# Gated linear attention: decay levels multiplied one head at a time, in half the rows, instead of two heads through a zero-padded operand

## The chip, the cores and the metric

The kernel runs on one core of one Trainium2 chip. The metric is device time of one launch in microseconds (us), the median of several runs. The engines are called PE (TensorE), DVE (VectorE), ACT (ScalarE), POOL (GpSimd) and SP (SyncE); PEld are PE's weight loads.

## The reference

A trunk of two layers over 512 positions of width 2048. Each layer normalises its input, projects it with one combined matrix, runs three head groups in parallel (a gated short convolution, stick-breaking attention with 8 heads, gated linear attention, GLA, with 4 heads of 64 keys and 128 values), multiplies each by a SiLU gate and projects the concatenation back into the residual stream. The GLA part, which is what changes:

```python
def step(state, inp):
    qc, kc, vc, gc = inp
    cum = jnp.cumsum(gc, axis=2)
    o_inter = jnp.einsum("bhck,bhkv->bhcv", qc * jnp.exp(cum), state)
    diff = cum[:, :, :, None, :] - cum[:, :, None, :, :]
    decay = jnp.where(causal, jnp.exp(jnp.minimum(diff, 0.0)), 0.0)
    att = jnp.einsum("bhtk,bhsk,bhtsk->bhts", qc, kc, decay)
    o_intra = jnp.einsum("bhts,bhsv->bhtv", att, vc)
```

and of the convolution `y = b_gate * (conv3(c_gate * h) + bias)`, times `silu(g)`.

## The kernel before

**Projections.** Activations lie in SBUF as two float16 halves (high and low), as do the weights (wh, wl), and every product is three matmuls (high by high, high by low, low by high). Weights come in blocks of 256 columns: POOL issues the load into `st`, ACT finds the sum of squares (L367), POOL reduces it over the partitions (L381), ACT writes wh (L436, L486), DVE writes wl (L443, L487). The plain projections are the matmuls at L673 to L675, L684 to L686 and L815; the ones at L765 and L768 belong to a scheme with seven products instead of eight (`project_quick`), which also needs sums of blocks. Two layers run one after the other: GLA's projections, the first half of the convolution, four pairs of attention heads, the second half of the convolution, the output projection.

**GLA.** Two head pairs p per layer, the two heads of a pair on partitions 0 to 63 and 64 to 127. Within blocks of 128 positions the decay between two positions is split by levels h = 64, 32, ..., 1 (`LEV`): at level h, a source in the first half of a stretch of 2h positions meets a target in the second half, and both decays are taken against the middle, so each factor stays at most 1. At each level DVE and ACT make e (L1045 to L1054), split the source into float16 halves in tile `qp` (`split_src`, L1009 and L1010) and the target into tile `th` (`split_tgt`, L1018 and L1019). The target tile has room for two heads beside each other: head 0's rows fill the columns h = 0, head 1's rows the columns h = 1, and the rest stays at the zeros that POOL wrote at the layer's start (L966). So one matmul over all 128 rows (`mm3`, L1024) gives both heads' scores, 64 target columns each, in one PSUM bank; 4 blocks by 3 terms make 12 of them a level. DVE writes what belongs to the level into `attd` under a mask (L1059). The diagonal comes from a matmul with `heads` (L1073) and a masked write (L1077). Decays between the blocks go through `mm3` with two and four blocks of targets at once, 256 and 512 columns. L1119 multiplies the scores with the values, `norm` (from L1121) normalises and gates.

**The first convolution** runs at the same time as the second head pair: `conv_in` puts h (times its scale) into tile `qT`, multiplies the c projection onto it, and convolves into `kT`; `conv_out` makes the gate in a tile `g`, of which there are two, and multiplies. The GLA gates `gg` hold the same two "g" tiles until their heads are normalised and stored (`mixsplit`).

**What sets the order.** After a start-up whose DVE and ACT order is written by hand, a scheduler that simulates the timeline sets the order of the instructions on each engine, with some priorities and hooks for the weights' preparation. Tiles of one tag share the buffers of that tag, so a tag also sets who waits for whom.

Of the kernel before, what the change touches and what calls it, by code (L numbers as in the profile page):

```python
# [17 lines left out]
P = 128  # L18
# [25 lines left out]
def hybrid_trunk(ctx, tc, x, norm_g, w_in, conv_w, conv_b, sb_qn_g, sb_kn_g,  # L44
# [33 lines left out]
    def wk(shape, tag, bufs=None, dt=F32):  # L78
        return work.tile(shape, dt, tag=tag, name=nm(tag), bufs=bufs)
# [46 lines left out]

    LEV = [64, 32, 16, 8, 4, 2, 1, 0]
    masks = const.tile([P, len(LEV), P], U8, tag="masks", name="masks")

    def make_masks():  # L130
        bits = wk([P, 2, P], "e", dt=I32)
        V.tensor_copy(bits[:, 0, :], colno)
        V.tensor_copy(bits[:, 1, :], pno.to_broadcast([P, P]))
        V.tensor_tensor(bits[:, 0, :], bits[:, 0, :], bits[:, 1, :], ALU.bitwise_xor)
        far = bits[:, 1, :].bitcast(F32)
        V.tensor_copy(far, bits[:, 0, :])
        V.tensor_scalar(bits[:, 1, :], bits[:, 1, :], 0x7F800000, None, ALU.bitwise_and)
        for li, h in enumerate(LEV):
            V.tensor_scalar(masks[:, li, :], far, float(h), None, ALU.is_equal)
# [113 lines left out]
    gmx = sm(depth, "gmx")  # L253
# [33 lines left out]
    def layer_consts():  # L287
# [3 lines left out]
        for l in range(depth):  # L291
# [3 lines left out]
            gq = sm(2, "kg")  # L295
# [239 lines left out]
    ssq = sm(NT * NG, "ssq").rearrange("p (t g) -> p t g", g=NG)  # L535
# [121 lines left out]
    for l in range(depth):  # L657
# [164 lines left out]
        def project_gate(mx=None, logistic=False):  # L822
# [3 lines left out]
            def dst():  # L826
                g.append(wk([P, 2, seq], "g"))
                return g[0]
# [136 lines left out]
        for a in scr:  # L965
            G.memset(a, 0.0)  # L966
        src16 = [[scr[0][:, b, i, :] for i in range(2)] for b in range(2)]
        tgt16 = [[scr[1][:, b, i, :].rearrange("p (t h c) -> p t h c", t=NT, h=2) for i in range(2)] for b in range(2)]
# [5 lines left out]
        for tag in ("qT", "kT"):  # L974
            o = wk([P, 2, seq], tag)
            ps, u = project(True, lambda: o)
            mx = sm(2, tag + "mx")
            for c in range(2):
                V.tensor_reduce(mx[:, c:c + 1], ps[c], AX.X, ALU.max, apply_absolute_value=True)
            gm = allmax(mx, 2, tag)  # L980
            m = sm(1, tag + "m")
            V.tensor_tensor(m, gm[:, 0:1], gm[:, 1:2], ALU.max)
            p2 = sm(1, tag + "p2")
            pow2(p2, m, -14.0, tag)
            s_ = sm(1, tag + "s")
# [26 lines left out]
        def split_tgt(e, b):  # L1012

            for hh in range(2):
                hs = slice(hh * HT, (hh + 1) * HT)
                eh = e[hs].rearrange("p (g c) -> p g c", c=HT)
                hi, lo = (a[hs, :, hh, :] for a in tgt16[b])
                S.activation(hi, eh, AF.Copy)  # L1018
                V.tensor_tensor(lo, eh, hi, ALU.subtract)  # L1019

        def mm3(o, sb, ss, tb, g0, g1):

            for i, (a, b) in enumerate(((0, 0), (0, 1), (1, 0))):
                T.matmul(o, src16[sb][a][:, ss], tgt16[tb][b][:, g0:g1].rearrange("p g h c -> p (g h c)"),  # L1024
                         start=i == 0, stop=i == 2)

        tsl = [slice(t * P, (t + 1) * P) for t in range(NT)]
        for p in range(2):
            Pp, q_, k_ = Pc[:, p, :], gq[:, p, :], gk[:, p, :]
            attd = wk([P, NT, 2, P], "zw")  # L1030
            G.memset(attd, 0.0)

            for li, h in enumerate(LEV[:-1]):
# [25 lines left out]
                V.copy_predicated(  # L1059
                    attd.rearrange("p t h (b s j) -> p (t h) b s j", s=2, j=h)[:, :, :, 1, :],  # L1060
                    masks[:, li, :].rearrange("p (o b s j) -> p o b s j", o=1, s=2, j=h)[:, :, :, 1, :].to_broadcast(
                        [P, 2 * NT, HT // h, h]),
                    aps.rearrange("p (t b j) -> p t b j", t=2 * NT, j=h))
# [7 lines left out]
            for t in range(NT):  # L1071
                for i, a in enumerate((hi, lo)):
# [3 lines left out]
            S.activation(own, aps, AF.Copy, scale=2.0 ** 14)  # L1076
            V.copy_predicated(attd.rearrange("p t h c -> p (t h) c"),  # L1077
                              masks[:, len(LEV) - 1:len(LEV), :].to_broadcast([P, 2 * NT, P]),
# [16 lines left out]
            for i in range(NT):  # L1095
                S.activation(att16[0][:, i], attd[:, i], AF.Copy, scale=2.0 ** -21)
                V.scalar_tensor_tensor(att16[1][:, i], attd[:, i], 2.0 ** -21, att16[0][:, i], ALU.mult, ALU.subtract)
# [7 lines left out]
            for a, o in zip(ax, (aps[:, 0], aps[:, 1], aps2[:, 0])):  # L1105
                S.activation(a[:, 0], o, AF.Copy, scale=2.0 ** -21)
                V.scalar_tensor_tensor(a[:, 1], o, 2.0 ** -21, a[:, 0], ALU.mult, ALU.subtract)
            ops2 = bank2()
            for hh in range(2):
# [3 lines left out]
                for t, cs, a, g0, g1 in ((0, tsl[1], ax[0], 0, 2), (2, tsl[3], ax[0], 2, 4),  # L1113
                                         (0, slice(256, 512), ax[1], 0, 4), (1, slice(256, 512), ax[2], 0, 4)):
                    seqmm.append((cs, t, [a[:, i].rearrange("p (g h c) -> p g h c", h=2, c=HT)[:, g0:g1, hh, :]
# [28 lines left out]
        def weight_ratio():  # L1144
# [8 lines left out]
            rp = sm(1, "rpm")  # L1153
# [10 lines left out]
        def conv_in(j, then=lambda: None):  # L1164
# [23 lines left out]
            return y  # L1188

        def conv_out(j, y, then=lambda: None):  # L1190

            g, u = project_gate(logistic=j == 1)
# [21 lines left out]
        conv_out(0, conv_in(0, lambda: norms.pop(0)()))  # L1214
# [70 lines left out]
        for j in range(4):  # L1285
# [15 lines left out]
            m = sm(1, "sbm")  # L1301
# [5 lines left out]
            for n in range(2):  # L1307
# [20 lines left out]
                u2 = sm(1, "qu2")  # L1328
# [28 lines left out]
        conv_out(1, conv_in(1, go), go)  # L1357
# [7 lines left out]
        if not last:  # L1365
            xt = [newbig("x", [P, 2, D], F32, l) for _ in range(2)]
            ssq = sm(NT * NG, "ssq").rearrange("p (t g) -> p t g", g=NG)
# [76 lines left out]
```

## Time and profile before

| | |
|---|---|
| median of 3 runs | 1662.28 us (1662.23 to 1664.69) |
| profiled execution | 1665.0 us, of which the span from the first to the last instruction 1663.1 us |
| granted TensorE clock, mean | 0.997 |
| PE matmuls, weight loads | 17098 each |
| DVE, ACT busy | 1393.4 us, 1181.9 us |
| DMA | 232.71 MB, mean 140 GB/s |

Busy time is the union of an engine's records. Matmuls are pipelined, so a record of a matmul is longer than the distance to the next one's start; rates are read from starts.

### The profile page before, as it was taken

To read this page: it belongs to the slowest core of one execution; us is meant where nothing else is said; L and a number is where in the kernel's file an instruction comes from. 1 tells how busy PE (TensorE), PEld (TensorE's weight loads), DVE (VectorE), ACT (ScalarE), POOL (GpSimd) and SP (SyncE) were. 2 spreads that over 40 slices of the span, in tenths; PEclk is the share of its full clock that TensorE was granted. 3 is DMA by queue.
4 is the path that set the end of the run, shared out by engine and by line. 5 is a ranking of instruction groups with operands and counts; after the bars stand their busy time and mean duration, and the time that the engine had idled before them with its cause. 6 is when DMAs were issued, how large, how long until landed. Compare 5 with 4: busy or idle time off the path is not lost.

```text
span 1663.1 us, 39967 instructions
## 1 busy us (share of the span) xinstructions
PE 1637.7 (98%) x17098; PEld 1327.7 (80%) x17098; DVE 1393.4 (84%) x2347; ACT 1181.9 (71%) x1739; POOL 257.8 (16%) x298
## 2 busy tenths in 40 slices
PE   7999999999999999999999999999999999999999
PEld 5746548989898967799996465689898989668998
DVE  8977789979898979897599686998888888788893
ACT  8667787877777776755675786888786867676571
POOL 1121012111212121011111110112121212111110
PEclk9999999999999999999999999999999999999999
DMA  7144324577776868456433433436677776783441
GB/s 259 52 153 113 102 64 87 132 155 144 162 151 156 157 153 204 154 162 207 163 103 104 112 104 107 121 83 176 115 167 146 160 152 136 155 240 127 153 154 52
DMA packets 189747, 232.71 MB, mean 140 GB/s; under 512 B 90162, under 2 KB 149884, under 8 KB 189056
## 3 DMA queue, kind: packets, MB, share of 16 engines
q0 software_dynamic: 72832, 175.12, 39.0%
q1 hardware_dynamic: 107728, 45.56, 13.4%
q10 hardware_dynamic: 9008, 9.45, 1.7%
q8 instruction: 134, 2.20, 0.5%
q14 instruction: 45, 0.37, 0.1%
HBM read 179.65 MB, written 14.68 MB: 117 GB/s over the span
## 4 chain that ended last, share of the span: by engine, by line
PE 65%; DVE 17%; DMA 8%; issue 4%; ACT 4%; POOL 1%; DVEq 0%; ACTq 0%; POOLq 0%
PE psp L768 14%; PE psp L674 7%; PE psp L673 7%; PE psp L675 7%; PE psp L685 5%; PE psp L686 5%; PE psp L684 5%; PE psp L765 5%; DMA st<-in_w_in_dram 5%; PE psp L815 5%; DMA th<-za 3%; DVE za L1251 2%; DVE wl L487 2%; DVE w7l L487 2%; DVE zw L1253 1%
## 5 line engine op out<-in xcount | busy, mean ns | idle before, releaser
L486 ACT ACTIVATE wh<-st,ws 128x1024 f16<-128x1024 f32 x222 | 247.8, 1146 | 192.2 <-DVE st L507 100.5
L487 DVE SCALAR_TENSOR_TENSOR wl<-st,ws,wh 128x1024 f16<-128x1024 f32 x222 | 279.6, 1280 | 31.5 <-ACT wh L486 31.2
L367 ACT ACTIVATE junk<-st 128x2048 uint8<-128x2048 f32 x150 | 285.3, 1902 | 12.8 <-DMA st<-in_w_in_dram 7.5
L443 DVE SCALAR_TENSOR_TENSOR wl<-st,ws,wh 128x2048 f16<-128x2048 f32 x78 | 182.8, 2349 | 28.2 <-ACT wh L436 27.1
L685 PE MATMUL psp<-wl,m 128*128 128x256 f16 x704 | 191.9, 273 | 0.0
L684 PE MATMUL psp<-wh,m 128*128 128x256 f16 x704 | 191.9, 273 | 0.0
L686 PE MATMUL psp<-wh,m 128*128 128x256 f16 x704 | 191.9, 273 | 0.0
L436 ACT ACTIVATE wh<-st,ws 128x2048 f16<-128x2048 f32 x76 | 151.0, 1995 | 50.8 <-DVE ws L397 24.2
L768 PE MATMUL psp<-wh,s 128*128 128x128 f16 x2048 | 176.9, 219 | 0.0
L768 PE MATMUL psp<-wl,s 128*128 128x128 f16 x1024 | 173.3, 219 | 0.0
L768 PEld LDWEIGHTS <-s 128*128 128x128 f16 x3072 | 173.1, 98 | 0.0
L381 POOL PARTITION_ALL_REDUCE wgm<-wm x75 | 42.3, 564 | 746.9 <-ACT junk L367 731.7
L355 POOL DMA_DIRECT2D st<-in_w_in_dram x114 | 101.8, 898 | 337.4 <-DVE wl L443 175.1
L765 PE MATMUL psp<-s,wh 128*128 128x256 f16 x896 | 151.9, 273 | 0.0
L765 PEld LDWEIGHTS <-wh 128*128 128x128 f16 x1344 | 131.4, 98 | 16.1 <-issue 1.0
L768 PEld LDWEIGHTS <-m 128*128 128x128 f16 x2160 | 124.3, 99 | 5.5 <-issue 5.0
L765 PE MATMUL psp<-s,wl 128*128 128x256 f16 x448 | 122.0, 273 | 0.0
L675 PEld LDWEIGHTS <-wl 128*128 128x128 f16 x576 | 56.4, 98 | 67.5 <-DVE wl L443 1.6
L675 PE MATMUL psp<-x,wl 128*128 128x512 f16 x288 | 109.0, 379 | 0.4 <-DVE wl L443 0.4
L674 PEld LDWEIGHTS <-wh 128*128 128x128 f16 x576 | 56.4, 98 | 66.3 <-issue 1.3
L674 PE MATMUL psp<-x,wh 128*128 128x512 f16 x288 | 109.2, 379 | 0.0
L674 PE MATMUL psp<-m,wh 128*128 128x512 f16 x288 | 109.2, 379 | 0.0
(426 smaller groups left out, 4195.4 us busy)
## 6 DMA issues: line engine op xcount, KB each, us to landing
st<-in_w_in_dram POOLq DMA_DIRECT2D x114, 1024.0 KB, 8.3
st<-in_w_out_dram POOLq DMA_DIRECT2D x32, 1024.0 KB, 8.4
st<-st POOLq DMA_DIRECT2D x30, 512.0 KB, 7.5
st<-in_w_in_dram SPq DMA_DIRECT2D x6, 1024.0 KB, 11.7
mixd<-g POOLq DMA_DIRECT2D x24, 256.0 KB, 6.2
x<-in_x_dram SPq DMA_DIRECT2D x4, 1024.0 KB, 4.9
qT<-in_x_dram ACTq DMA_DIRECT2D x8, 512.0 KB, 3.7
qT<-xs ACTq DMA_DIRECT2D x8, 512.0 KB, 4.2
```

Source lines behind the costliest of these rows:

```text
L367: sq = S.activation(junk(HK * GW).rearrange("p (k n) -> p k n", k=HK), staged[i][h], AF.Square, accum_out=peak[i][:, h:h + 1])
L436: hi = S.activation(wh[:, :, :GW], staged[i][h], AF.Copy, scale=scales[i])
L443: V.scalar_tensor_tensor(wl[:, :, :GW], staged[i][h], scales[i], wh[:, :, :GW], ALU.mult, ALU.subtract)
L486: hi = S.activation(h_, b, AF.Copy, scale=sc)
L487: V.scalar_tensor_tensor(l_, b, sc, h_, ALU.mult, ALU.subtract)
L674: T.matmul(o, wh[:, kk, cs], xl[:, :, k, :], start=False, stop=False)
L675: mm = T.matmul(o, wl[:, kk, cs], xh[:, :, k, :], start=False, stop=en)
L684: T.matmul(o, ah[:, t, k, :], wh[:, kk, :n], start=st_, stop=False, skip_group_check=True)
L685: T.matmul(o, ah[:, t, k, :], wl[:, kk, :n], start=False, stop=False, skip_group_check=True)
L686: return T.matmul(o, al[:, t, k, :], wh[:, kk, :n], start=False, stop=en, skip_group_check=True)
L765: mm = T.matmul(o, w[q_][:, kk, :], a[p_][:, :, kk, :], start=st_, stop=en, skip_group_check=True)
L768: mm = T.matmul(o[:, t * P:(t + 1) * P], a[p_][:, t, kk, :], w[q_][:, kk, :], start=st_, stop=en, skip_group_check=True)
```

## The change

The target halves become plain tiles of 128 rows and half the columns. `mm3` issues, for each term, one matmul for each head, over that head's 64 rows of source and target, into that head's own PSUM bank. `attd` changes its layout from (block, head, column) to (head, block, column), the masks hold only the second halves of each stretch, four blocks wide, and the diagonal has a mask of its own. Only the source tile is still zeroed. The first convolution's gate is written over its h values. Several small tiles of one to four columns now share tags, among them those of the q and k projections' maxima.

```diff
-    masks = const.tile([P, len(LEV), P], U8, tag="masks", name="masks")
+    masks = const.tile([P, len(LEV) - 1, NT, P // 2], U8, tag="masks", name="masks")
+    mdiag = const.tile([P, P], U8, tag="mdiag", name="mdiag")
...
-        for li, h in enumerate(LEV):
-            V.tensor_scalar(masks[:, li, :], far, float(h), None, ALU.is_equal)
+        for li, h in enumerate(LEV[:-1]):
+            V.tensor_scalar(masks[:, li].rearrange("p t (b j) -> p t b j", j=h),
+                            far.rearrange("p (o b s j) -> p o b s j", o=1, s=2, j=h)[:, :, :, 1, :].to_broadcast(
+                                [P, NT, HT // h, h]), float(h), None, ALU.is_equal)
+        V.tensor_scalar(mdiag, far, 0.0, None, ALU.is_equal)
...
-        def project_gate(mx=None, logistic=False):
+        def project_gate(mx=None, logistic=False, room=None):
...
-                g.append(wk([P, 2, seq], "g"))
+                g.append(room or wk([P, 2, seq], "g"))
...
-        for a in scr:
-            G.memset(a, 0.0)
+        G.memset(scr[0], 0.0)
         src16 = [[scr[0][:, b, i, :] for i in range(2)] for b in range(2)]
-        tgt16 = [[scr[1][:, b, i, :].rearrange("p (t h c) -> p t h c", t=NT, h=2) for i in range(2)] for b in range(2)]
+        tgt16 = [[scr[1][:, b, i, :seq // 2] for i in range(2)] for b in range(2)]
...
-            mx = sm(2, tag + "mx")
+            mx = sm(2, "gamx")
...
         def split_tgt(e, b):
-            for hh in range(2):
-                hs = slice(hh * HT, (hh + 1) * HT)
-                eh = e[hs].rearrange("p (g c) -> p g c", c=HT)
-                hi, lo = (a[hs, :, hh, :] for a in tgt16[b])
-                S.activation(hi, eh, AF.Copy)
-                V.tensor_tensor(lo, eh, hi, ALU.subtract)
+            hi, lo = tgt16[b]
+            S.activation(hi, e, AF.Copy)
+            V.tensor_tensor(lo, e, hi, ALU.subtract)
 
         def mm3(o, sb, ss, tb, g0, g1):
             for i, (a, b) in enumerate(((0, 0), (0, 1), (1, 0))):
-                T.matmul(o, src16[sb][a][:, ss], tgt16[tb][b][:, g0:g1].rearrange("p g h c -> p (g h c)"),
-                         start=i == 0, stop=i == 2)
+                for hh in range(2):
+                    hs = slice(hh * HT, (hh + 1) * HT)
+                    T.matmul(o[:, hh, :], src16[sb][a][hs, ss], tgt16[tb][b][hs, g0 * HT:g1 * HT], start=i == 0,
+                             stop=i == 2, skip_group_check=True)
...
-            attd = wk([P, NT, 2, P], "zw")
+            attd = wk([P, 2, NT, P], "zw")
...
-                aps = bank2()[:, 0, :]
+                aps = bank2()[:, :, :NT * HT]
                 for t in range(NT):
-                    mm3(aps[:, tsl[t]], b, tsl[t], b, t, t + 1)
+                    mm3(aps[:, :, t * HT:(t + 1) * HT], b, tsl[t], b, t, t + 1)
...
-            mm3(aps[:, 0, :256], 0, tsl[0], 0, 0, 2)
-            mm3(aps[:, 0, 256:], 0, tsl[1], 0, 2, 4)
-            mm3(aps[:, 1, :], 1, tsl[0], 1, 0, 4)
+            mm3(aps[:, :, :128], 0, tsl[0], 0, 0, 2)
+            mm3(aps[:, :, 128:256], 0, tsl[1], 0, 2, 4)
+            mm3(aps[:, :, 256:], 1, tsl[0], 1, 0, 4)
             aps2 = bank2()
-            mm3(aps2[:, 0, :], 1, tsl[1], 1, 0, 4)
+            mm3(aps2[:, :, :256], 1, tsl[1], 1, 0, 4)
...
-            return y
+            return y, None if j else hb
...
-            g, u = project_gate(logistic=j == 1)
+            g, u = project_gate(logistic=j == 1, room=room)
...
-        conv_out(0, conv_in(0, lambda: norms.pop(0)()))
+        conv_out(0, *conv_in(0, lambda: norms.pop(0)()))
```

The scheduler places every engine's instructions anew. Two places show how. On PE, in layer 0's first head pair, the last level stands before among the projection's matmuls (L673 to L675, x times wh or wl); L1024 are the level matmuls, and the name `psz` is their bank pair:

```order
L675 MATMUL psp_2373<-x_184,wl_1562 128x512
L1024 LDWEIGHTS qp_986
L1024 MATMUL psz_1863<-th_987,qp_986 128x128
L673 LDWEIGHTS wh_1561
L673 MATMUL psp_2374<-x_184,wh_1561 128x512
L674 LDWEIGHTS wh_1561
L674 MATMUL psp_2374<-x_185,wh_1561 128x512
L1024 LDWEIGHTS qp_986
L1024 MATMUL psz_1887<-th_987,qp_986 128x128
L675 LDWEIGHTS wl_1562
```

After the change the same place reads as follows (L1027 are the level matmuls, L678 to L680 the projection's):

```order
L679 MATMUL psp_2529<-x_186,wh_1560 128x512
L1027 LDWEIGHTS qp_987
L1027 MATMUL psz_1944<-th_988,qp_987 128x64
L1027 LDWEIGHTS qp_987
L1027 MATMUL psz_1944<-th_988,qp_987 128x64
L680 LDWEIGHTS wl_1561
L680 MATMUL psp_2529<-x_185,wl_1561 128x512
L678 LDWEIGHTS wh_1560
```

A single matmul of 128 columns among the projection's has become a pair of 64 columns, one for each head, and the projection goes on around it.

On DVE, in layer 0's second head pair, before (L1010 and L1019 split source and target, L1045 and L1046 make e, L851 belongs to the first convolution's gate):

```order
L1010 TENSOR_TENSOR qp_986<-e_2115,qp_986 128x16x16
L1019 TENSOR_TENSOR th_987<-e_2115,th_987 64x4x64 x2
L851 SCALAR_TENSOR_TENSOR ga_2787<-g_2785,ga_2787 128x512
L1010 TENSOR_TENSOR qp_986<-e_2141,qp_986 128x32x8
L1045 TENSOR_TENSOR e_2167<-raw_941 128x256
L1046 TENSOR_TENSOR e_2167<-raw_941 128x256
L1019 TENSOR_TENSOR th_987<-e_2141,th_987 64x4x64 x2
```

And after (L1014, L1020, L1048, L1049 and L856 are the same steps, L1062 writes a level into `attd`, L448 makes a weight block's low half):

```order
L856 SCALAR_TENSOR_TENSOR ga_2949<-qT_2524,ga_2949 128x512
L1014 TENSOR_TENSOR qp_987<-e_2212,qp_987 128x16x16
L1020 TENSOR_TENSOR th_988<-e_2212,th_988 128x256
L1062 COPY_PREDICATED zw_2138<-masks,psz_2186 128x16x32
L1048 TENSOR_TENSOR e_2284<-raw_942 128x256
L1049 TENSOR_TENSOR e_2284<-raw_942 128x256
L448 SCALAR_TENSOR_TENSOR wl_3002<-st_2817,ws_2997,wh_3001 128x8x256
L1014 TENSOR_TENSOR qp_987<-e_2248,qp_987 128x32x8
```

Two target splits over 64 partitions have become one over 128, the gate reads the h values' tile (qT in place of g) and stands one split earlier, and the weights' low half stands between the two levels.

More of the change, by code (lines that the diff above doesn't have):

```diff
@@ L1075, in hybrid_trunk @@
             own = sm(2 * NT, "own")
[L1076 to L1078 removed]
+            S.activation(own.rearrange("p (h t) -> p t h", h=2), aps.rearrange("p (t h) -> p t h", h=2), AF.Copy,
+                         scale=2.0 ** 14)
+            V.copy_predicated(attd.rearrange("p h t c -> p (h t) c"),
+                              mdiag.rearrange("p (o c) -> p o c", o=1).to_broadcast([P, 2 * NT, P]),
                               own.rearrange("p (a o) -> p a o", o=1).to_broadcast([P, 2 * NT, P]))
```

48 lines of the change are left out of this document (25 added, 23 removed).

## The prediction

> **What bounds the kernel now.** I read the page's busy line first, then the waits of TensorE, then two long windows around the stages that the change touches.
>
> ```profile
> PE 1637.7 (98%) x17098; PEld 1327.7 (80%) x17098; DVE 1393.4 (84%) x2347; ACT 1181.9 (71%) x1739; POOL 257.8 (16%) x298
> ```
>
> ```profile
> PE psp L768 <- DVE kT L781: 7.0, 5, 2.0
> PE psz L239 <- DVE identb L221: 3.6, 1, 3.6
> ...
> PE psz L1119 <- DVE za L1107: 0.4, 2, 0.2
> ...
> PE psp L675 <- DVE wl L443: 0.4, 1, 0.4
> ```
>
> ```profile
> core 0: us, PE busy (x) PEld busy (x) DVE busy (x) ACT busy (x) POOL busy (x), PEclk, DMA share, GB/s
> 100.00:280.00 180.00, 180.00 (x1203) 107.30 (x1201) 148.01 (x299) 135.67 (x212) 22.25 (x28) 1.00 0.35 101
> 680.00:1090.00 410.00, 410.00 (x3670) 307.35 (x3669) 332.27 (x562) 284.24 (x383) 56.02 (x69) 1.00 0.41 126
> ```
>
> TensorE (PE) is busy for 98% of the span. A busy PE could still be a slow one, because the records overlap, so I check its rate below by start-to-start distances. Its waits are short: the largest is 7.0 us in five places of the attention stage (L768), another 3.6 us is start-up. The whole of layer 0's GLA stage lies in 100 to 280 us, that of layer 1 in 680 to 1090 us: there PE is busy in every microsecond, at clock 1.00, with 0.2 us of waits for the last GLA product of each layer (L1119, 0.4 us in two times). So in the stages that are changed, VectorE (DVE) and ScalarE (ACT) set nothing; a microsecond added to PE or taken from it is a microsecond of the kernel.
>
> **The price of a matmul there.** The level matmuls and their neighbours in the timeline of PE, and the last wide ones in the chain (start, length, pieces):
>
> ```profile
> 148.09 1.28 PE L1024 MATMUL psz<-th,qp 128*128 128x128 f16 x20
> 149.21 0.27 PE L765 MATMUL psp<-x,wh 128*128 128x256 f16 x1
> ...
> 184.19 0.32 PE L1073 MATMUL psz<-heads,qp 128*128 128x2 f16 x7
> 184.37 0.81 PE L1024 MATMUL psz<-th,qp 128*128 128x256 f16 x6
> 185.02 0.38 PE L674 MATMUL psp<-x,wh 128*128 128x512 f16 x1
> ```
>
> ```profile
> 189.50 1.29 PE psz L1024 x6
> ```
>
> ```profile
> L1024 PEld LDWEIGHTS <-qp x384: 95/98/98, 148.0 to 1090.1; 128*128 128x128 f16 x192
> L1024 PE MATMUL psz<-th,qp x384: 219/219/379, 148.1 to 1090.3; 128*128 128x128 f16 x168, 128*128 128x256 f16 x12, 128*128 128x512 f16 x12
> ```
>
> Twenty matmuls of 128 columns take 149.21 - 148.09 = 1.12 us, 56 ns each; six of 256 columns 0.65 us, 108 ns each; six of 512 1.29 us, 215 ns each; seven of 2 columns 0.18 us, 25.7 ns each. These fit columns / 2.4 + 2.6 ns with a floor near 25.5 ns. The weight load of 98 ns is hidden in all of them. Per layer and head pair there are 84 level matmuls of 128 columns (7 levels x 4 blocks x 3 terms), 6 of 256 and 6 of 512. Four such sets make the 384 of the row: 336 x 0.056 + 24 x 0.108 + 24 x 0.215 = 18.8 + 2.6 + 5.2 = 26.6 us of PE.
>
> **Part 1: the levels by head.** Each matmul over 128 rows and n columns (half of its target is zero) becomes two, one over rows 0 to 63 into one PSUM bank, one over rows 64 to 127 into the other, n / 2 columns each. So 672 of 64 columns, 48 of 128, 48 of 256.
>
> Streaming, two bounds. *In turn*: 64 columns are 64 / 2.4 + 2.6 = 29.3 ns, so 672 x 0.0293 + 48 x 0.056 + 48 x 0.108 = 19.7 + 2.7 + 5.2 = 27.6 us, 1.0 us more than before. *At once* (the two heads share neither rows, nor weights, nor bank): the 64-column ones then stop at the floor of a start, 672 x 0.0257 = 17.3 us, the wide ones cost half of theirs, 1.3 + 2.6 = 3.9 us; 21.2 us, 5.4 us less. No row shows two matmuls at once. I take *at once* as likelier, because the two matmuls of a pair share no operand and stand side by side in the order, and keep both ends.
>
> A rule bears on this. The Trainium skill, TensorEngine Tiling (Array Packing), Theoretical Speedup, gives "Up to 2×" where the contracted dimension is at most 64; by that the 26.6 us would become 13.3, and with the switches below the sum -3.2; the first rival is this rule worked out from rows. The row of 25.7 ns per start speaks against it for 64 columns.
>
> Switching, a price that stands in this trace once. L289 is the one matmul in the warm part of the kernel that contracts fewer than 65 rows (42). It and its neighbours in the timelines of PE and of the weight loads; then, as control, a float32 transpose over 128 rows in the same surroundings:
>
> ```profile
> 28.36 0.71 PE L815 MATMUL psp<-wl,x 128*128 128x256 f16 x5
> 29.00 0.25 PE L289 MATMUL psm<-ident,e 42*128 42x42 f32 x1
> 29.19 0.61 PE L815 MATMUL psp<-wh,x 128*128 128x256 f16 x4
> ...
> 29.00 0.14 PEld L289 LDWEIGHTS psm<-ident,e 42*128 42x128 f32 x1 [0.21 <-issue]
> ```
>
> ```profile
> 22.25 0.71 PE L815 MATMUL psp<-wh,x 128*128 128x256 f16 x5
> 22.80 1.04 PE L562 MATMUL psz<-ident,x 128*128 128x128 f32 x8
> 23.67 0.60 PE L815 MATMUL psp<-wh,x 128*128 128x256 f16 x4
> ```
>
> In the control the fifth L815 starts at 22.25 + 4 x 0.109 = 22.69 and L562 0.11 later: no gap; each of its eight takes 0.87 / 8 = 0.109. Before L289 the fifth L815 starts at 28.80 and L289 0.20 later, 0.09 more than its 0.109; its weight load was not fetched ahead (0.21 of "issue" before it). After it, 0.19 us pass for a transpose of 42 columns, which at the control's rate needs 0.109 x 42 / 128 = 0.04: 0.15 more. So one trip from 128 rows to a part of the array and back costs about 0.24 us. Lower end 0.09 (only the first gap is the switch's), upper end 0.30 (L289's own work taken as nothing, and as much again as the first gap for a level's longer tail).
>
> How many trips there are follows from PE's order, of which the section on the change shows a place. Over the program the level matmuls stand in 44 unbroken runs before (128 rows like everything around them, so no switch) and in 42 after, of 2 to 48 matmuls, each with full-height matmuls ahead and behind. 42 x 0.24 = 10.1 us added, bounds 42 x 0.09 = 3.8 and 42 x 0.30 = 12.6.
>
> Sum of part 1 on PE: -5.4 + 10.1 = +4.7 us; in turn, +1.0 + 10.1 = +11.1.
>
> **Part 2: what DVE, ACT and POOL lose.**
>
> ```profile
> L1019 DVE TENSOR_TENSOR th<-e,th 64x256 f16<-64x256 f32 x72 | 30.0, 417 | 1.7 <-ACT th L1018 0.4
> L1018 ACT ACTIVATE th<-e 64x256 f16<-64x256 f32 x72 | 29.4, 409 | 7.0 <-DVE e L1054 3.8 <-DVE e L1091 2.3
> L1010 DVE TENSOR_TENSOR qp<-e,qp 128x256 f16<-128x256 f32 x32 | 13.5, 426 | 2.3 <-ACT qp L1009 1.8
> L966 POOL MEMSET th<- 128x2048 f16 x4 | 7.2, 1808 | 17.5 <-DMA m<-th 11.4 <-DVE e L132 6.1
> ```
>
> The target split needs 36 instructions on each of DVE and ACT instead of 72: L1010 shows that 128 partitions take 426 ns where 64 took 417. DVE gets back 72 x 0.417 - 36 x 0.426 = 14.7 us, ACT about as much (29.4 - 36 x 0.41 = 14.6), POOL four memsets of 1.81 us, 7.2 us. All of it lies beside PE work in the two windows where PE never stops, so it brings the span only the 0.4 us of L1119. The 7.0 us at L768 lie outside both windows, in the attention stage, whose own DVE work comes between. I count 0.
>
> In DVE's order of the second head pair, shown above, the gate moves ahead of a level and the weights' low half (L443, now L448) to behind one; DVE's waits there cost PE nothing as long as PE has projections to do.
>
> **Part 3: the gate's tile, masks, small tiles.** The first convolution's gate no longer needs a "g" tile that the GLA gates still hold; PE does not wait there, so 0. Its tile is freed later, when its copy has landed, and attention pair 1 takes it, more than four projections further on (96 matmuls of 512 columns, 20.6 us, is one of the first convolution's); without that cover it would cost the few us of a landing. The masks are seven of 256 columns and one of 128 instead of eight of 128:
>
> ```profile
> L139 DVE TENSOR_SCALAR masks<-e x8: 207/304/648, 95.8 to 97.3; 128x128 uint8<-128x128 f32 x8
> ```
>
> At twice the time that is at most 7 x 0.30 = 2.1 us of DVE, in layer 0, ahead of the GLA window, where PE's only wait after start-up is the 0.4 us at L675. The shared small tiles make k's maximum wait for q's to be read, one projection earlier. The level's masked write reads two banks instead of one, as many elements. I put 0 on these, and ±1 us for waits that a new order may bring.
>
> **Sum.** The profiled execution took 1665.0 us, of which the span is 1663.1; the median of the three timed runs is 1662.28, 2.7 us lower. 1665.0 + 4.7 = 1669.7 there; on the median's scale 1662.3 + 4.7 = **1667.0 us**. With the switch's bounds: -5.4 + 3.8 - 1 to -5.4 + 12.6 + 1, 1659.7 to 1670.5 for this case alone. 0.2%, about what a measurement of this kernel can tell from no change, is 3.3 us.
>
> **Rivals.**
> - *Weight loads pair up too (faster).* If the two heads' starts don't count against one floor, a pair of 64 columns costs 29.3 ns: 336 x 0.0293 + 3.9 = 13.7 us, 12.9 less; with the switches -2.8, 1659.5 us. For it: disjoint rows. Against: 25.7 ns per start in the L1073 row. Chance 0.12.
> - *The switch is free (faster).* The gaps at L289 would then belong to that instruction alone, and the sum is -5.4, 1656.9 us. For it: a single sample. Against: the control has no gap. It decides where a trip costs less than 5.4 / 42 = 0.13 us. Chance 0.10.
> - *In turn (slower).* Heads stream one after the other, and the switches come on top: +11.1, 1673.4 us. It decides where a pair of 64 columns takes more than about 56 ns. Chance 0.20.
> - *Weight loads in the open (slower by more).* 768 loads of 98 ns that nothing hides are 75 us in place of 26.6, with the switches +58, 1721 us. Against: 98 ns loads are hidden at 25.7 ns per start in the L1073 stretch. Chance 0.05. The Trainium skill, TensorE: Matmul & The Clock Gate, LDWEIGHTS, has a load cost by its columns and not by its rows, about 128 / 1.2 = 107 ns here; by that, halving the rows saves nothing on a load. The 98 ns agree; that it is hidden is this trace's.
> - *The relief of DVE shows.* Part 2's 15 us reach the L768 waits: up to -7.0 of them, against +4.7, 1660. Chance 0.03.
>
> **How the numbers follow.** The forecast has 0.50; of it 0.34 lie over 3.3 us above 1662.3, 0.15 within, 0.01 below. Slower: 0.34 + 0.20 + 0.05 = 0.59. Faster: 0.01 + 0.05 of the first rival, 0.09 of the free switch, 0.01 of the relief: 0.16. The rest, 0.25, within. The range takes the forecast's own lower end, with it the first rival's time, and the "in turn" case: 1659.0 to 1674.5. The free switch and the open loads stay out, 0.15 together.
>
> **What would show it.** Right: level matmuls of 64 columns about 26 ns apart within a run, the wide ones at 28 and 54 ns on average, and some 0.1 us missing at both ends of each run, with the next weight load not fetched ahead; PE still busy throughout 100 to 280 us, DVE and ACT some 15 us less busy each. Wrong: 29 ns and 56 / 108 ns apart (in turn); no gaps at the runs' ends; waits of PE for DVE at L1027, which would be the new order's doing; or L768's waits gone.

## The result

The changed kernel takes 1672.83 us (median of nine runs, 1666.90 to 1680.77) where the kernel before takes 1663.96 (1662.23 to 1664.94): ratio 1.0054, 95% interval 1.0040 to 1.0068. In a later series the same kernel took 1668.97 (twelve runs, 1663.82 to 1674.61) against 1663.84 (1661.44 to 1670.02): 1.0027 (1.0015 to 1.0039). So it is slower, by 5 to 9 us. Its runs lie 11 to 14 us apart, those of before 2.7 in the first series and 8.6 in the second.

The first profile is of the longest of the nine runs (1680.77 us, span 1679.0). I read it first for the two GLA windows, on which the prediction rested. The page's busy line, the two windows (columns as before the change), and TensorE's timeline at the first level of layer 0:

```profile
PE 1640.2 (98%) x17482; PEld 1318.8 (79%) x17482; DVE 1375.8 (82%) x2311; ACT 1166.4 (69%) x1703; POOL 253.3 (15%) x294
```

```profile
100.00:280.00 180.00, 180.00 (x1417) 103.10 (x1415) 142.78 (x289) 129.16 (x197) 22.68 (x29) 1.00 0.36 103
680.00:1090.00 410.00, 404.84 (x3798) 297.63 (x3796) 324.32 (x548) 273.82 (x359) 52.73 (x67) 1.00 0.43 131
```

```profile
148.98 0.27 PE L770 MATMUL psp<-s,wl 128*128 128x256 f16 x1
149.09 0.27 PE L770 MATMUL psp<-s,wh 128*128 128x256 f16 x1
149.29 0.49 PE L1027 MATMUL psz<-th,qp 64*128 64x64 f16 x22
149.72 0.28 PE L770 MATMUL psp<-x,wh 128*128 128x256 f16 x1
149.84 0.27 PE L770 MATMUL psp<-x,wl 128*128 128x256 f16 x1
```

Two things are seen at once. PE is still busy throughout 100 to 280 us, and a run of 22 level matmuls lasts 0.43 us (149.29 to 149.72). Before, 20 matmuls of 128 columns lasted 1.12 us; 22 of the new ones do the work of 11 of those, 0.62 us. A run of 48, a little later, lasts 0.81:

```profile
171.27 0.87 PE L1027 MATMUL psz<-th,qp 64*128 64x64 f16 x48
172.08 0.39 PE L679 MATMUL psp<-x,wh 128*128 128x512 f16 x1
```

So 13 pairs more take 0.38 us, 29 ns each. Of the 0.43, eleven pairs are 0.32, and about 0.1 is the way out of the run. On the way in, L1027 starts 0.20 after the L770 ahead of it, where the next-door L770s are 0.11 apart: 0.09 more. So the levels cost PE less than before, not more.

What got worse lies elsewhere. The waits of PE in the changed kernel (us in total, times, longest):

```profile
PE psp L773 <- DVE raw L793: 4.9, 2, 2.5
PE psp L689 <- ACT m L1164: 4.9, 1, 4.9
PE psp L773 <- DVE kT L786: 4.0, 5, 1.1
...
PE psp L689 <- DVE kT L1213: 2.5, 1, 2.5
...
PE psp L691 <- DVE m L1165: 1.8, 2, 1.2
```

L773 for L793 is attention pair 0, once in each layer. L689 and L691 are the first projections over the new mix, which wait for its rescaling (L1164, L1165) or for what stands behind that on DVE (L1213), and the rescaling waits for the loads of the mix's halves. None of these rows stood in the profile before; only the one for kT (L786) did, with 7.0.

To find where time comes and goes I used that all kernels of this study have the same 15840 projection matmuls on PE, nearly all in the same order (at most 160 of the places hold a matmul of another kind). The table says how much later the n-th of them starts than in the profile of before, counted from stretch to stretch (us; the times at the head are those of before, and the stretch up to 122 us, with -0.7 to +1.1, is left out):

```
stretch             GLA 0   pair 0  rest    mix 0   rest    GLA 1   attn 1  pair 0  rest    mix 1
from (us)           122     303     337     664     696     888     1116    1140    1168    1475
changed             -2.3    +5.2    -2.6    +6.7    +0.6    -3.2    +0.9    +4.5    -1.6    +6.5
changed, again      -2.3    +5.1    -2.6    +0.7    +0.4    -3.2    +0.9    +5.4    +0.4     0.0
levels alone        -3.0    +6.2    -1.2    +4.5    +0.4    -3.8    +0.9    +5.3    -2.3   +16.5
gate alone          -0.1    +0.9    +0.4     0.0    +0.9    -0.1    +0.9    +1.3    -2.7     0.0
small tiles alone    0.0     0.0    -0.2    +0.6    +1.5     0.0     0.0     0.0    -2.2     0.0
changed, add first  -2.3    +0.1    +0.4     0.0    +1.3    -3.2    +0.9     0.0    +7.3     0.0
levels, add first   -3.0     0.0    -1.3    +1.3    +0.9    -3.8    +0.9     0.0    -1.0     0.0
before, add behind   0.0    +4.4    -1.2    +1.7     0.0     0.0     0.0    +4.8    -1.2     0.0
```

The two columns GLA hold the gain of the change, 5.5 us together, the same to 0.1 in both profiles of the changed kernel. 0.9 of it is no gain: two matmuls of GLA's normalisation (L1127 before, L1132 after, 0.43 us each) stand ahead of the mark at 1116 before and behind it after, and come back as the +0.9 of the next column. So the change gains 2.3 us in each layer, 4.6 together. The profile of "levels alone" is of a run that counts as slow (1689.22 us, 1.5% above its fastest and left out of the ratio below), so only what other rows bear out is read from it. The two columns "pair 0" are a loss of some 10 us that comes back every time. The columns "mix" come and go: 13.2 us in the first profile, 0.7 in the second.

The loss at pair 0 starts on POOL's queue. Its timeline there, before and then after the change (each row is an issue or an all-reduce; the brackets say what POOL waited for):

```profile
307.91 0.40 POOL L381 PARTITION_ALL_REDUCE wgm<-wm  x1 [8.65 <-ACT junk L367]
308.42 1.60 POOL L504 DMA_DIRECT2D st<-st  x1
310.64 1.82 POOL L355 DMA_DIRECT2D st<-in_w_in_dram  x2 [0.62 <-DVE w7l L487]
```

```profile
308.03 1.77 POOL L360 DMA_DIRECT2D st<-in_w_in_dram  x2 [9.44 <-DVE w7l L492]
309.83 0.35 POOL L386 PARTITION_ALL_REDUCE wgm<-wm  x1
310.06 1.62 POOL L509 DMA_DIRECT2D st<-st  x1
```

`st<-st` is a DMA that adds one quarter of a weight block to another in SBUF; DVE needs its sum (L507 before, L512 after) to form the parts of k's weights. Before, it is issued ahead of the next two weight fetches of 1 MB each. In the changed kernel it is issued behind them, and DVE, in whose queue the copy L793 stands further back, waits for it. The add also takes longer there, 10.8 us from issue to landing instead of 7.8:

```profile
320.95 1.23 DVE L512 TENSOR_TENSOR st<-st 128x1024 f32<-128x1024 f32 x1 [3.68 <-DMA st<-st]
322.10 1.28 DVE L492 SCALAR_TENSOR_TENSOR wl<-st,ws,wh 128x1024 f16<-128x1024 f32 x1
323.29 1.22 DVE L514 TENSOR_TENSOR st<-st 128x1024 f32<-128x1024 f32 x1
324.43 1.28 DVE L492 SCALAR_TENSOR_TENSOR wl<-st,ws,wh 128x1024 f16<-128x1024 f32 x1
325.62 0.42 DVE L793 TENSOR_TENSOR raw<-psp,raw 128x256 f32<-128x256 f32 x1
```

Before, the same sum and the same copy:

```profile
317.49 1.22 DVE L507 TENSOR_TENSOR st<-st 128x1024 f32<-128x1024 f32 x1
323.66 0.42 DVE L788 TENSOR_TENSOR raw<-psp,raw 128x256 f32<-128x256 f32 x1
```

What let the fetches pass is the split of q's weights on DVE, which frees the buffer that they wait for. Its row and that of the first step that uses the all-reduce (L384, then L389), before, and then after:

```profile
308.34 0.16 DVE L384 TENSOR_TENSOR wq<-wgm 128x1 f32<-128x1 f32 x1 [0.64 <-POOL wgm L381]
308.91 1.28 DVE L487 SCALAR_TENSOR_TENSOR w7l<-st,ws,w7h 128x1024 f16<-128x1024 f32 x1
```

```profile
306.46 1.28 DVE L492 SCALAR_TENSOR_TENSOR w7l<-st,ws,w7h 128x1024 f16<-128x1024 f32 x1
312.87 0.15 DVE L389 TENSOR_TENSOR wq<-wgm 128x1 f32<-128x1 f32 x1
```

The split starts 2.45 us earlier, of which 1.2 are PE's lead at that place, and it now stands ahead of the steps that use the all-reduce instead of behind them. So the fetches come up first. The order on the queue is fixed when the program is built.

### The profile page after: what moved, and what is told of

The parts are those of the page before. It is cut to its first block, busy times and chain, and to the rows that moved or that the text cites. A ratio compares the mean times of both kernels' runs of the same rounds, so it can differ in the third digit from the quotient of the medians.

```text
span 1679.0 us, 40628 instructions
## 1 busy us (share of the span) xinstructions
PE 1640.2 (98%) x17482; PEld 1318.8 (79%) x17482; DVE 1375.8 (82%) x2311; ACT 1166.4 (69%) x1703; POOL 253.3 (15%) x294
## 5 line engine op out<-in xcount | busy, mean ns | idle before, releaser
L491 ACT ACTIVATE wh<-st,ws 128x1024 f16<-128x1024 f32 x222 | 248.8, 1149 | 190.5 <-DVE st L512 91.4
L448 DVE SCALAR_TENSOR_TENSOR wl<-st,ws,wh 128x2048 f16<-128x2048 f32 x78 | 182.8, 2348 | 29.9 <-ACT wh L441 29.5
L689 PE MATMUL psp<-wh,m 128*128 128x256 f16 x704 | 193.4, 275 | 7.4 <-ACT m L1164 4.9
L691 PE MATMUL psp<-wh,m 128*128 128x256 f16 x704 | 193.6, 275 | 1.8 <-DVE m L1165 1.8
L773 PE MATMUL psp<-wh,s 128*128 128x128 f16 x2048 | 180.0, 221 | 6.1 <-DVE raw L793 4.9
L773 PEld LDWEIGHTS <-s 128*128 128x128 f16 x3072 | 176.0, 99 | 6.6 <-issue 6.6
L773 PE MATMUL psp<-wl,s 128*128 128x128 f16 x1024 | 175.8, 221 | 0.0
L770 PE MATMUL psp<-s,wh 128*128 128x256 f16 x896 | 151.7, 273 | 0.0
L770 PEld LDWEIGHTS <-wh 128*128 128x128 f16 x1344 | 131.4, 98 | 16.8 <-issue 1.6
L773 PEld LDWEIGHTS <-m 128*128 128x128 f16 x2160 | 123.0, 98 | 5.2 <-issue 4.8
L770 PE MATMUL psp<-s,wl 128*128 128x256 f16 x448 | 122.0, 273 | 0.0
L680 PEld LDWEIGHTS <-wl 128*128 128x128 f16 x576 | 56.3, 98 | 67.8 <-DVE wl L448 1.6
L680 PE MATMUL psp<-x,wl 128*128 128x512 f16 x288 | 109.2, 379 | 0.4 <-DVE wl L448 0.4
L680 PE MATMUL psp<-m,wl 128*128 128x512 f16 x288 | 109.2, 379 | 0.0
```

The costliest lines, as they stand in the source:

```text
L448: V.scalar_tensor_tensor(wl[:, :, :GW], staged[i][h], scales[i], wh[:, :, :GW], ALU.mult, ALU.subtract)
L491: hi = S.activation(h_, b, AF.Copy, scale=sc)
L680: mm = T.matmul(o, wl[:, kk, cs], xh[:, :, k, :], start=False, stop=en)
L689: T.matmul(o, ah[:, t, k, :], wh[:, kk, :n], start=st_, stop=False, skip_group_check=True)
L691: return T.matmul(o, al[:, t, k, :], wh[:, kk, :n], start=False, stop=en, skip_group_check=True)
L770: mm = T.matmul(o, w[q_][:, kk, :], a[p_][:, :, kk, :], start=st_, stop=en, skip_group_check=True)
```

## The experiments

**The changed kernel again.** No edit; a second profile, of a run near the median (1670.42 us).

> The changed kernel once more, for a second profile. The first profile had PE stalls outside the GLA windows: 2.6 + 0.9 us at 322 us and 2.6 + 0.6 at 1148 (L773 behind DVE's L793), 5.0 us at 684 and some 4.7 us at 1510 (the loads of the mix halves landing late). Theory A (the new order of POOL's queue, two weight fetches ahead of the accumulating DMA, makes the stalls at 322 and 1148; they are fixed by the order): both come back within 0.5 us, median 1668 to 1675. Theory B (all of it is transfers that happen to be late): they come and go, and a profile of a faster execution has none of them. For the stalls at 684 and 1510 both leave open whether they come back; if they do not, they are the spread of 14 us between executions.

Measured: 1668.97 us, 1.0027 (1.0015 to 1.0039). The waits for L793 are the same as in the first profile, to the digit (the whole loss at pair 0 of layer 1 is 5.4 us instead of 4.5); those for the mix halves are down to 0.4 us:

```profile
PE psp L773 <- DVE raw L793: 4.9, 2, 2.5
...
PE psp L773 <- ACT wh L491: 1.9, 2, 0.9
...
PE psp L689 <- ACT m L1164: 0.4, 2, 0.2
```

So two different things are at work: theory A's stall, fixed by the order, and late mix halves that only some executions have. From here on the sums go by this profile. It also shows what a stall of 2.5 us costs. TensorE's windows before, in and after the time that follows the wait (the column PEclk is the third from the right):

```profile
318.00:322.00 4.00, 4.00 (x75) 4.00 (x73) 1.29 (x2) 1.42 (x4) 0.00 (x0) 1.00 0.51 109
325.90:328.60 2.70, 2.70 (x27) 2.70 (x27) 2.70 (x4) 2.70 (x4) 0.00 (x0) 0.50 0.00 0
329.00:333.00 4.00, 4.00 (x75) 4.00 (x73) 3.93 (x12) 2.54 (x14) 1.85 (x3) 1.00 0.02 4
```

PE starts no matmul for 1.1 us more than usual from 322.0 (0.9 of them the wait for the weights of L491) and for 2.6 from 323.2 (the wait for L793), and after that it runs at clock 0.50 for 2.8 us, in which matmuls of 128 columns are 107 ns apart in place of 56: 27 x 0.051 = 1.4 us more. 1.1 + 2.6 + 1.4 = 5.1, the number in the table.

**Levels alone.** The changed kernel, its masks and shared small tiles with it, but the first convolution's gate keeps a tile of its own.

```
-            return y, None if j else hb
+            return y, None
```

> The levels by head, with their masks and small tiles, but the first convolution's gate in a tile of its own as before. Theory A (the levels' new order brings the inversion in POOL's queue at 308 us, which this kernel has too): stalls at 322 and 1148 of 3 to 3.6 us each, and on PE in the GLA windows 4 us less than before; 1665 to 1673. Theory C (the gate written over h makes the stalls): 4.4 us faster than before, about 1659.5, and no stall at 322.

Measured: 1675.62 us (1664.25 to 1689.22), 1.0058 (1.0037 to 1.0080). The row "levels alone": 6.2 and 5.3 us lost at pair 0, 6.8 gained in the GLA columns (0.9 of them the same two matmuls), and late mix halves of 4.5 and 16.5 us in the profiled run, the longest of the ten. The median lies 2.6 us over the range that theory A gave; late halves may be why, but only the profiled run shows them. Theory C falls: the stall is there without the gate over h.

**Gate alone.** The kernel before, with the gate written over h and nothing else.

```
-                g.append(wk([P, 2, seq], "g"))
+                g.append(room or wk([P, 2, seq], "g"))
...
-            return y
+            return y, None if j else hb
```

> The kernel before with the first convolution's gate written over its h values and nothing else. POOL's queue keeps the accumulating DMA ahead of the two weight fetches. Theory A: no stall at 322, within 2 us of before. Theory C (the gate's tile makes the loss): 8 to 13 us slower, 1672 to 1677, with the stalls.

Measured: 1667.11 us (1665.91 to 1673.37), 1.0025 (1.0013 to 1.0038). No wait for raw and no loss of 5 us at pair 0. But the gate is not free: 3.3 us by the medians, where theory A said within 2. From the column GLA to pair 0 the profile has 0.8 us more in layer 0 and 2.1 in layer 1. Among PE's waits, the copies of kT on ACT have grown; they stood at 2.2 us in six times with the small tiles alone:

```profile
PE psp L768 <- ACT kT L784: 4.2, 8, 1.1
```

One of 0.9 and one of 1.1 us lie just there. I did not follow these small waits further.

**Small tiles alone.** The kernel before, with the tags of the small tiles shared as in the changed one, for instance:

```
-            mx = sm(2, tag + "mx")
+            mx = sm(2, "gamx")
```

> The kernel before with the small tiles shared as in the changed kernel and nothing else. Theories A and C: within 1.5 us of before. Theory D (k's maximum waits for q's to be read, and other waits of shared small tiles delay the chains of scales): 3 us or more slower, with new waits for the tiles of the scales.

Measured: 1664.16 us, 0.9999 (0.9991 to 1.0008). Theory D falls, and the 0 that the prediction gave these tiles was right.

**The add first.** The changed kernel, with the one order on POOL's queue given back: for attention q of pair 0 the next fetch is emitted after the add of k's weights, and ordered behind it.

```
-        G.dma_start(out=b12, in_=b11, accum_op=ALU.add)
+        added[0] = G.dma_start(out=b12, in_=b11, accum_op=ALU.add)
...
-            queue.dma_start(s_, src[l, h * HK * P:(h + 1) * HK * P, c0:c0 + GW].rearrange("(k p) n -> p k n", p=P),
+            a = queue.dma_start(s_, src[l, h * HK * P:(h + 1) * HK * P, c0:c0 + GW].rearrange("(k p) n -> p k n", p=P),
...
+            if i - 2 in behind:
+                order(a, added[0])
```

> The changed kernel with one order given back on POOL's queue, in each layer once: the accumulating DMA of the weights of k of attention pair 0 is issued ahead of the two weight fetches, as it stands in the kernel before. Theory A (that inversion makes the stalls at 322 and 1142 us): both stalls go, and PE is 5.1 + 5.3 us ahead of the repeat's profile at those places; median about 1669.0 - 10.4 = 1658.6, so faster than before by 0.3%. Theory E (the stalls come from DVE being behind there for another reason, the DMA's lateness being incidental): they stay within 1 us, median 1667 to 1670.

Measured: 1659.47 us (1657.27 to 1668.74), 0.9965 (0.9949 to 0.9981): faster than before, and 0.9 us from theory A's number. POOL's timeline (line numbers are 4 to 8 higher in this kernel):

```profile
306.37 0.40 POOL L392 PARTITION_ALL_REDUCE wgm<-wm  x1 [9.56 <-ACT junk L378]
306.89 1.60 POOL L517 DMA_DIRECT2D st<-st  x1
307.82 2.49 POOL L364 DMA_DIRECT2D st<-in_w_in_dram  x2
```

DVE's wait for the sum is 1.3 us in place of 3.7, and the row "changed, add first" has +0.1 and 0.0 in the columns pair 0. What is left, 5.0 us under before by the medians, is about the 4.6 that the levels gain. The 7.3 us further on in that row belong to the profiled run, the longest of the ten: there DVE waits 6.6 us for another such sum until 1427.7 us, and later ACT 3.2 us for a transpose (`th<-za`).

**Levels alone, the add first.** The same order in the kernel with the gate's own tile.

> The same order given back in the kernel that has the levels by head but keeps the gate's own tile. Theory A: no stall at 322 and 1142, so 10.4 us under that kernel without late mix halves (about 1669), 1656 to 1660; late mix halves at 685 and 1510, if they belong to the levels and not to the stall at 322, still cost 5 to 16 us in some executions. Theory E: as without the order, 1665 to 1676.

Measured: 1658.06 us (1655.29 to 1665.19), 0.9959 (0.9944 to 0.9973). It is the fastest of all, 6.4 us under before; against the one with the gate over h the medians differ by 1.4 us, which the intervals do not separate. Late mix halves cost its profile 1.3 us at the first mix and nothing at the second.

**Before, the add behind.** The opposite edit, on the kernel before, with no level and no gate touched: the add is ordered behind the two fetches.

```
-        G.dma_start(out=b12, in_=b11, accum_op=ALU.add)
+        a = G.dma_start(out=b12, in_=b11, accum_op=ALU.add)
+        if i - 1 in behind:
+            order(a, fetched[0])
```

> The kernel before with that one order turned round on POOL's queue: the accumulating DMA is issued behind the two weight fetches. No level, gate or tile is changed. Theory A: stalls of 2.5 to 6 us appear at 322 and 1140, 5 to 12 us slower than before, 1669 to 1676. Theory E: within 2 us of before.

Measured: 1674.76 us (1672.86 to 1679.50), 1.0054 (1.0034 to 1.0074). POOL's timeline, the wait of DVE for the sum in layer 0, and the wait of PE for the copy behind it in both layers (lines 5 to 7 higher than in the kernel before):

```profile
308.48 0.40 POOL L386 PARTITION_ALL_REDUCE wgm<-wm  x1 [8.65 <-ACT junk L372]
311.06 1.79 POOL L360 DMA_DIRECT2D st<-in_w_in_dram  x2 [2.18 <-DVE w7l L492]
312.85 1.61 POOL L509 DMA_DIRECT2D st<-st  x1
```

```profile
DVE st L514 <- DMA st<-st: 4.9, 1, 4.9
```

```profile
PE psp L775 <- DVE raw L795: 4.5, 2, 2.4
```

One order turned round in each layer makes the whole loss, 10.3 us by the medians; 4.4 and 4.8 us stand at pair 0 in the profile. With "the add first" the cause is shown from both sides; theory E falls.

**The price of a switch.** The changed kernel with 84 further matmuls of 64 columns between the blocks of the levels, into columns that nobody reads, once over 128 rows and once over rows 0 to 63.

```
+                    if t < NT - 1:
+                        T.matmul(whole_[:, 0, NT * HT:NT * HT + HT], src16[b][0][:, tsl[t]],
+                                 tgt16[b][0][:, t * HT:(t + 1) * HT], start=True, stop=True, skip_group_check=True)
```

> The changed kernel with a further matmul over all 128 rows, 64 columns, between every two blocks of a level (3 x 28 = 84 in all), into columns of the bank that nobody reads. Its twin has the same matmul over rows 0 to 63 only, so that the row mode doesn't change. If a change of mode costs 0.20 us a trip, as the ends of the runs show, this one has 84 x 0.20 = 16.8 us more than the twin in the two GLA windows and about 19 us more there than the changed kernel; if the switch is free and the gaps at the ends of runs belong to the neighbours, it has 84 x 0.03 = 2.5 us more than the changed kernel and as much as the twin.

> The twin of the kernel with full-height matmuls between the blocks: the same 84 further matmuls of 64 columns at the same places, over rows 0 to 63 only, so that no mode changes within a run. The full-height one stood 19.6 us over the repeat of the changed kernel in the two GLA windows (9.7 + 9.8). If the change of mode is the cost, this one stands 84 x 0.029 = 2.5 us over it there; if the price is that of any further matmul with its weight load, it stands 15 to 20 us over it as well.

Measured, in the two GLA stretches against the changed kernel's -5.5 us: +14.0 with the full-height ones, -4.0 with the half-height ones, that is 19.5 and 1.5 us more (each kernel ran once, so the stretches are compared and not the times). 19.5 / 84 = 0.23 us each, less 0.03 for streaming 64 columns: 0.20 us per trip from half rows to full rows and back. The trip is seen in the timeline of PE, here of the first level with the full-height ones (L1064):

```profile
147.68 0.26 PE L1027 MATMUL psz<-th,qp 64*128 64x64 f16 x6
147.87 0.20 PE L1064 MATMUL psz<-th,qp 128*128 128x64 f16 x1
148.01 0.26 PE L1027 MATMUL psz<-th,qp 64*128 64x64 f16 x6
```

Six matmuls in three pairs take 0.19 us to the start of L1064, 0.10 over 3 x 0.029; L1064 takes 0.14, 0.11 over its 0.03.

**Heads apart.** The changed kernel with three matmuls of one head, then three of the other, instead of pairs.

```
-            for i, (a, b) in enumerate(((0, 0), (0, 1), (1, 0))):
-                for hh in range(2):
+            for hh in range(2):
+                for i, (a, b) in enumerate(((0, 0), (0, 1), (1, 0))):
```

> The changed kernel with the six matmuls of a block in another order: three of the one head, then three of the other, instead of pairs. If the two row halves run at once and each half works in turn, a block of 64 columns takes 4 slots of 29 ns instead of 3 and the wide ones 4 instead of 3: 112 x 0.029 = 3.3 us and 4 x (2 x 0.056 + 2 x 0.108) = 1.3 us more, with two more runs (0.4) 5.0 us more in the two GLA windows. If neighbours of different heads gain nothing from standing side by side, 0 to 0.4 us more.

Measured: -3.9 us in the GLA stretches, 1.6 more than the changed kernel, of which two more runs are 0.4. Neither expectation holds: the 5.0 us are not there, and yet the heads do run at once. The run of 22 is 0.46 us long (0.43 in pairs), one step of 29 ns more; at four steps a block it would be 0.53, and with the heads in turn over 0.64:

```profile
149.06 0.52 PE L1027 MATMUL psz<-th,qp 64*128 64x64 f16 x22
149.52 0.28 PE L770 MATMUL psp<-x,wh 128*128 128x256 f16 x1
```

So a matmul of one row half does not wait for the three of the other half that stand ahead of it; the neighbourhood of the pairs is not what makes the gain. The rest of the 1.6 us I have not followed.

**One fetch behind the mix halves.** The changed kernel, with the weight fetch that POOL issues at 664.8 and 1490.6 us put on SP's queue behind the last load of the mix halves.

```
-        queue = nc.gpsimd if i > 2 else nc.sync
+        queue = nc.gpsimd if i > 2 and i - 2 not in onsp else nc.sync
...
+            if i - 2 in onsp:
+                order(a, lastload[0])
```

> The changed kernel (with the inversion on POOL's queue still in it) with one weight fetch of each layer, that which POOL issues at 664.8 and 1490.6 us, moved to SP's queue behind the last load of the mix halves. It says nothing on the stalls at 322 and 1142, which stay. If the late mix halves (landing 17 us and more after issue, PE stalls of 5 to 16 us at 684 and 1510 in some executions) come from that fetch running beside the transposes and the loads: the loads land within 10 us, no execution has these stalls, median 1667 to 1670 and the spread of the executions falls from 11 to 17 us to under 7. If the lateness has another source: landings of 12 to 18 us and a spread of over 10 us as before; and if the fetch comes too late for its own use, a new stall of a few us near 690 and 1515.

Measured: 1668.55 us (1663.67 to 1673.20), 1.0024 (1.0013 to 1.0036). The DMA view of 640 to 690 us, first of the changed kernel's first profile, then of its second, then of this one (KB each, us from issue to landing):

```profile
m<-mixd SPq DMA_DIRECT2D x2, 768.0 KB, 17.9
...
m<-mixd SPq DMA_DIRECT2D x2, 256.0 KB, 17.1
```

```profile
m<-mixd SPq DMA_DIRECT2D x2, 768.0 KB, 14.3
...
m<-mixd SPq DMA_DIRECT2D x2, 256.0 KB, 12.9
```

```profile
m<-mixd SPq DMA_DIRECT2D x2, 768.0 KB, 6.3
...
m<-mixd SPq DMA_DIRECT2D x2, 256.0 KB, 4.8
```

The loads of the first mix land in 5 to 6 us; for the second the view has no landing. The profile loses nothing at either mix, but so little is lost with landings of 13 to 14 us too (0.7 us in the second profile of the changed kernel). And the spread is 9.5 us, against 10.8 of the changed kernel in its second series, where I had said under 7: this execution, the longest of its twelve, lost 4.2 us near 1350 us instead, where PE waits 2.2 us for a transpose (`kT<-qp`). So without the fetch beside them these loads landed earlier in the one profile that there is; that the fetch makes the stalls at the mix is not shown, and it is not the only source of the spread. Why transfers are late in some executions and not in others stays open.

## Why the prediction was right and wrong

The number held: 1672.83 and 1668.97 lie within 1659.0 to 1674.5, near 1667.0, and slower was the likeliest sign. But that is luck. The mechanism did not hold: I had the 4.7 us come from the levels on PE, and there the change gains 4.6; a loss at pair 0 that I had put at nothing, 10.5 us, makes up for it.

- **What bounds the kernel.** Right: in the GLA stretches a microsecond of PE is one of the kernel. The gain of 2.3 us a layer is what the prices below add up to, and DVE's 17.6 and ACT's 15.5 us less brought nothing in these stretches.
- **Streaming, -5.4.** Wrong, and the first rival was right, to which I gave 0.12. A pair of 64 columns costs 29 ns, so 336 x 0.0293 + 3.9 = 13.7 us and -12.9, as its working says (the wide ones, 56 and 109 ns a pair, went as forecast). The step that failed is the floor of 25.7 ns per start. The L1073 row had it for matmuls over all rows, and I carried it over to matmuls on different rows. The Trainium skill, TensorEngine Tiling (Array Packing), Key Properties, says "Tiles operate independently"; the heads that run at once even when three of one stand ahead of the other agree.
- **Switching, +10.1.** Right in kind, close in size: 0.20 us a trip instead of 0.24, so 42 x 0.20 = 8.4. The same section of the Trainium skill has a change of mode drain the engine, without a price; this trace gives one. Together -12.9 + 8.4 = -4.5, the rival's -2.8 with the measured trip; the table has -4.6 without the two matmuls of L1127. The kernel with the gate's own tile has 36 runs instead of 42 and is 1.3 us lower in these columns, for 6 x 0.20 = 1.2. The upper end of 0.30 does not follow from its two terms, which give 0.28 and, with the first gap once more, 0.37; the measured 0.20 lies under either.
- **Part 2, DVE's relief counted 0.** I asked what the relief brings in the windows, and not what DVE would reach earlier. In the new order, q's weight split stands 2.45 us earlier on DVE, and two fetches pass the add on POOL's queue. That the levels bring this order is shown (levels alone have it, the gate alone and the small tiles alone do not); that it is DVE's relief that does it is my reading of the orders and was not tried by itself.
- **Part 3, 0 with ±1 for waits that a new order may bring.** This is where the sum broke: 10.5 us at pair 0, and 10.3 by the medians where only this order is turned round. I had looked at PE's order and DVE's around the gate, and not at POOL's, where the turned pair could be read. The gate itself, at 0, measured 3.3 us alone; the shared small tiles, at 0, measured 0.3.
- **The sum, by the second profile:** -4.6 in the GLA stretches, +10.5 at pair 0, -0.4 all else: +5.5, where its span is 5.6 over that of before (1668.7 and 1663.1).
- **In turn, the free switch, the open weight loads:** fallen, by the 0.43 us of a run, the 0.20 us of a trip, and the same run. **Relief that shows** is not settled: the waits of L773 for kT on DVE are 4.0 and 4.5 us in the two profiles against 7.0 before, but 5.6 with the small tiles alone, where DVE is not relieved; and the stretch after pair 0 of layer 0 has -2.6 in both profiles of the changed kernel, but also -1.2 in the kernel before with the add behind, where DVE is not relieved, and +0.4 with the add first, where it is.

## What to carry to other kernels

When a change has every instruction placed anew, look at what each engine now releases earlier, one that bounds nothing included, and read the order of every queue that is fed by it, the DMA queues first: two large fetches that slip ahead of one small transfer can cost more than the change is worth, and one order given back turned a loss of 5 us into a gain of 5. Splitting a contraction whose operand is half zero into two row halves pays if the runs are long: here a pair of 64 columns saves 27 ns against the 56 of the matmul that it replaces, and a trip between half and full rows costs 0.20 us, so by my estimate a run must hold eight pairs or more.

## What the runs showed of the hardware that I had not expected

- Two matmuls of 64 columns on different row halves, with their weight loads, take 29 ns together, and need not alternate: three of one half, then three of the other, run as fast within 0.03 us per 22 matmuls.
- A trip from full rows to half rows and back costs 0.20 us, about 0.1 at either end.
- Waits of 1.1 and 2.6 us with one matmul between them were enough for the clock to fall to 0.50: in the second profile from 325.35 to 328.76 us, so that 2.8 us of the matmuls behind them ran slow, in the first from 327.48, 1.4 us after PE had started again. The Trainium skill, TensorE: Matmul & The Clock Gate, Part 1: The HAM clock gate, has the clock fall after an idle window of about 3.4 us; the two gaps together are 3.7, but no single one is that long in either profile, so the trace agrees only if the one matmul between does not count.
- Executions of one kernel lie up to 14 us apart here (the changed one, 1666.90 to 1680.77). In the profiles of the longest executions transfers land late at different places: the mix halves in one, a sum of weight quarters near 1428 us in another, a transpose near 1350 us in a third.
